# Up weights with turned signs: pair sums by additions and an adding DMA, h's operands moved by 128 bytes, and a cut second product

## The chip, the cores and the metric

The kernel runs on one core of a Trainium2 chip. The metric is the device time of one execution in microseconds (us), the median of several runs. A core has a matrix engine (TensorE, "PE" in the profile, with its weight loads as "PEld"), a vector engine (VectorE, "DVE"), a scalar engine (ScalarE, "ACT"), a general engine (GpSimd, "POOL") and a queue engine (SyncE, "SP") that issues plain DMAs. DMAs that add to what they find at their destination are issued by POOL here. Matrix products read two operands from on-chip memory (the loaded one is called "weights", the streamed one "moving") and write into one of eight accumulation banks.

## The reference

One layer of a bidirectional encoder on x of shape (1, 512, 1024), all in float32:

```python
x = x + 0.5 * swiglu(rms_norm(x, g1), w_gate1, w_up1, w_down1)   # 1024 -> 2752 -> 1024
h = rms_norm(x, g_mix);  u = h @ w_in
x = x + concat([fourier(u), attention(u)]) @ w_out
x = x + 0.5 * swiglu(rms_norm(x, g2), w_gate2, w_up2, w_down2)   # 1024 -> 2752 -> 1024
y = rms_norm(x, g_final)
# swiglu(h, g, u, d) = (silu(h @ g) * (h @ u)) @ d
```

The change touches the two SwiGLU blocks only.

## The kernel before, in words

Every product of two float32 matrices is done with split operands. A value is cast to the engine's short float form (the high part), and what the cast lost is the low part. `product` issues three matmuls: high weights times high, high weights times low, low weights times high. So each weight tile costs a DMA, a cast for the high part (mostly on ACT, L147, L343, L352) and a subtraction for the low part (mostly on DVE, `lows`, L118).

`ffn` does one SwiGLU block. The 2,752 hidden columns are 21 chunks of 128 and a tail of 64. Chunks are worked in four groups. The first group uses plain products on all 512 positions. In the other three groups, `seven` computes the gate and the up product of a chunk together as a "pair", by a scheme of seven half-size products instead of eight. The two weight matrices of the pair make a 2 by 2 block matrix (a11 and a12 are the upper and lower half of the gate chunk's 1,024 rows, a21 and a22 those of the up chunk), and the activations make another (b11, b12, b21, b22: halves of rows and of positions). The scheme needs four sums of weight blocks (s1 to s4) and four of activation blocks (t1 to t4, made once by `operands` and kept in `rt`). Each of the seven steps multiplies one weight block with one activation block: 4 row chunks times 3 split products are 12 matmuls of 128x128 weights with 256 moving columns, so a pair is 84 matmuls, all recorded at line L382 (`multiply`). Steps run in the order 0 (a11, bank r), 1 (a12, bank p2), the previous pair's step 9 (a22, its bank r), 3 (s1, bank q), 4 (s2, bank r), 5 (s4, bank q), 6 (s3, bank r). Between steps ACT copies partial results out of the banks (p1, p5, u2 by `kept`, L390; u at L418 and L426), applies silu (L414), and DVE adds and multiplies (L403, L413, L419, L427). The last pair's step 9 has no following pair; it is run by `rest` after the first down product of the group and is called the tail step below.

`prepare` makes the weights of a pair one pair ahead. It issues the DMAs of the gate and the up chunk (512 KB each) and returns a list of pieces: `both` casts two blocks into a high and a low slot, `single` does one block, and `combine` makes one of the four sums on DVE (L358). `PIECES` says how many pieces are handed out after each step. Weights live in a ring of 12 slots of 128x1024: eight of them (`own`) belong to the pairs in these stages, four (`shared`) also serve the down weights. A slot is taken by `take` and given back after the last step that reads it. `take(most)` prefers the own slots, except that for the last but one preparation of a stage it prefers the shared ones for everything but a11/a12.

After the pair stage of a group, `down` multiplies the finished activations (tile `at`) with eight tiles of down weights (products of 512 columns, L155 to L157), and `residual` (L468) adds each result to x. The first pair of the next group is prepared during these down products.

PE and SP execute in program order (`in_order`). On ACT, DVE and POOL a scheduler chooses the order when the kernel is built. All waits follow from who reads and writes a tile or a slot.

Lines to know: `ffn` 250 to 542, `operands` 296, `take` 319, `prepare` 330, `multiply` 376, `step` 393, the loop with the hand-out of pieces 432 to 445, `down` 447, the group loop 473 to 542. `room(pool, n)` places the next tile of a pool at address n modulo 256 bytes; the ring lies at 128, `at` at 128, `rt` at 192.

Of the kernel before, what the change touches and what calls it, by code (L numbers as in the profile page):

```python
# [6 lines left out]
F32 = mybir.dt.float32  # L7
# [6 lines left out]
P = 128  # L14
# [16 lines left out]
USES = "a11", "a12", "s1", "s2", "s4", "s3", "a22"  # L31
PIECES = (0, 2, 2, 1, 1, 1, 1)
KH = KD // 2
HI_DVE = ("f0", "f1")
SWAP_DMA = ("q1", "q2", "q3")
# [44 lines left out]
def encoder(ctx, tc, A, out):  # L80
# [169 lines left out]
    def ffn(norm, after, wgu, wd, wdt, groups, opening, closing):  # L250
# [6 lines left out]
        with tc.tile_pool(name=f"act{n_}", bufs=1) as ap, tc.tile_pool(name=f"sums{n_}", bufs=2) as sp:  # L257
            room(ap, 192)
            at = ap.tile([P, PLACES, 2, S], F32R, name=f"at{n_}")
            room(ap, 64)  # L260
            rt = ap.tile([P, 7, 2, KH, HALF], F32R, name=f"rt{n_}")
# [34 lines left out]
            def operands(rp, i0, i1):  # L296
                for i in range(i0, i1):
                    b = sp.tile([P, 4, HALF], F32, tag="raw_g", name=f"b{n_}_{i}")
                    for o, k in ((0, i), (2, i + KH)):
                        nc.vector.scalar_tensor_tensor(  # L300
                            out=b[:, o : o + 2].rearrange("p a b -> p (a b)"), in0=x[k],
                            scalar=gains[:, norm.n, k : k + 1], in1=rp, op0=ALU.mult, op1=ALU.mult,
                        )
                    b12, b11, b22, b21 = (b[:, o] for o in range(4))
                    t = sp.tile([P, 4, HALF], F32, tag=("s12", "s34")[i % 2], bufs=1, name=f"t{n_}_{i}")
                    for o, (p, q) in enumerate(((b12, b11), (b22, t[:, 0]), (b22, b12), (b21, t[:, 1]))):
                        nc.vector.tensor_tensor(out=t[:, o], in0=p, in1=q, op=ALU.subtract)
                    for src, c in ((b[:, 1:], slice(0, 3)), (t, slice(3, 7))):
                        h, l = rt[:, c, 0, i], rt[:, c, 1, i]
                        nc.scalar.copy(h, src)  # L310
# [18 lines left out]

            def prepare(j, most=False):  # L330

                g = sp.tile([P, KD * P], F32, tag="raw_g", name=f"raw_g{n_}_{j}")
                u = wp.tile([P, KD * P], F32, tag="raw", name=f"raw_u{n_}_{j}")
                for t, c in ((g, 2 * j), (u, 2 * j + 1)):
                    nc.sync.dma_start(out=t.rearrange("p (a b) -> p a b", b=P), in_=wgu[c])
                a11, a12, a21, a22 = g[:, :S], g[:, S:], u[:, :S], u[:, S:]
                s12 = sp.tile([P, 2 * S], F32, tag="s12", bufs=1, name=f"s12_{n_}_{j}")
                s34 = sp.tile([P, 2 * S], F32, tag="s34", bufs=1, name=f"s34_{n_}_{j}")
                w = {}

                def both(names, src):
                    hi, lo = (take(most and names[0] != "a11") for _ in range(2))
                    nc.scalar.copy(hi, src)  # L343
                    lows(lo, src, hi)
                    for i, n in enumerate(names):
                        w[n] = tuple(t[:, i * S : (i + 1) * S] for t in (hi, lo))
                    w[max(names, key=USES.index), "slots"] = hi, lo

                def single(n, src):
                    t = take(False)  # L350
                    hi, lo = t[:, :S], t[:, S:]
                    nc.scalar.copy(hi, src)  # L352
                    lows(lo, src, hi)
                    w[n] = hi, lo
                    w[n, "slots"] = (t,)

                def combine(out, a, b, op):
                    nc.vector.tensor_tensor(out=out, in0=a, in1=b, op=op)  # L358
# [12 lines left out]
            def seven(js, done):  # L371
# [3 lines left out]

                def multiply(ps, wn, on, w, first):

                    (whi, wlo), (mhi, mlo) = w[wn], (part[on][:, i] for i in range(2))
                    for i in range(KH):
                        ks = slice(i * P, (i + 1) * P)  # L380
                        for o, (a, b) in enumerate(((whi, mhi), (whi, mlo), (wlo, mhi))):
                            nc.tensor.matmul(  # L382
                                ps, a[:, ks], b[:, i], start=first and i == 0 and o == 0,
                                stop=i == KH - 1 and o == 2, skip_group_check=not first,
                            )
                    give(*w.get((wn, "slots"), ()))
# [6 lines left out]
                def step(j, w, n):  # L393
                    b = banks.setdefault(j, {})
                    if n == 0:
                        b["r"] = bank(f"r{n_}_{j}")[:, :HALF]
                        multiply(b["r"], "a11", "b11", w, True)
                        b["p1"] = kept(b["r"], "p1", j)
# [16 lines left out]
                    elif n == 6:  # L415
                        multiply(b["r"], "s3", "t3", w, False)
                        b["u"] = tp.tile([P, S], F32, tag="u", name=f"u{n_}_{j}")
                        nc.scalar.copy(b["u"][:, :HALF], b["r"])  # L418
                        nc.vector.tensor_tensor(  # L419
                            out=b["u"][:, :HALF], in0=b["u"][:, :HALF], in1=b["p5"], op=ALU.add  # L420
                        )
                    elif n == 9:
                        multiply(b["r"], "a22", "t4", w, False)
                        u, i = b["u"], place(j)
                        h, l = at[:, i, 0], at[:, i, 1]
                        nc.scalar.copy(u[:, HALF:], b["r"])  # L426
                        nc.vector.tensor_tensor(out=u, in0=b["g"], in1=u, op=ALU.mult)  # L427
# [4 lines left out]
                for s in range(7 * len(js)):  # L432
# [40 lines left out]
            for gi, group in enumerate(groups):  # L473
# [36 lines left out]
                for d in range(KD):  # L510
# [920 lines left out]
```

## Time and profile before

| what | value |
|---|---|
| runs shown | 856.64, 856.88, 858.42 us; median 856.88 |
| profiled execution, span from first to last instruction | 855.1 us, 1.8 below the median of the runs |
| granted TensorE clock, mean | 0.996 |
| PE busy | 846.4 us (99%) in 5,434 matmuls |
| DVE busy | 641.5 us (75%) |
| ACT busy | 467.9 us (55%) |
| POOL busy | 33.3 us (4%) |
| DMA | 89.25 MB, 28.6% of the engines on SP's queue, 3.2% on POOL's |
| matmuls of the pairs (L382) | 2,940 of 128x256, 381.5 us of records |
| matmuls of the down products (L155, L156, L157) | 900 of 128x512, 350.7 us of records |

The profile is that of one execution. Records of neighbouring matmuls overlap, because a matmul's record runs until its result is out while the next one has started; so the distance between two starts, not the length of a record, is the price of one matmul in a stream. A row of the timeline gives the start, the length and the operation, and `x12` means that twelve of them follow each other. Where an engine was idle before a row, the time and what ended it stand in brackets.

### The profile page before, as it was taken

How to read it: one execution, taken by the hardware profiler on the slowest of the kernel's cores; microseconds unless marked ns; L12 is line 12 of the kernel's file. 1: busy time of each engine (PE TensorE's matmuls, PEld its weight loads, DVE VectorE, ACT ScalarE, POOL GpSimd, SP SyncE). 2: the span in 40 equal slices, each digit the busy share in tenths (PEclk: the TensorE clock that was granted, in tenths of full speed). 3: DMA queues.
4: the chain of work that ended last, by engine and by line, in shares of the span. 5: the costliest groups of instructions: out<-in, count | busy, mean ns of one | idle time of the engine just before them, and what ended most of it. 6: DMA issues, size and time to landing. Idle time of an engine off the chain costs nothing.

```text
span 855.1 us, 13706 instructions
## 1 busy us (share of the span) xinstructions
PE 846.4 (99%) x5434; PEld 765.5 (90%) x5434; DVE 641.5 (75%) x1007; ACT 467.9 (55%) x781; POOL 33.3 (4%) x35
## 2 busy tenths in 40 slices
PE   9999999999999999999999999999999999999996
PEld 7878998899989998889988888899989998899986
DVE  7998985488756937699999478999846985488453
ACT  7763764266524635677776347656632764266352
POOL 0110000000000000222000000100000000000001
PEclk9999999999999999999999999999999999999998
DMA  6664322323243113414020224553232331323213
GB/s 250 164 157 157 118 88 74 118 99 127 74 145 109 48 56 111 148 50 136 26 74 26 99 70 116 120 196 108 77 117 100 118 106 56 117 100 113 67 43 99
DMA packets 31424, 89.25 MB, mean 104 GB/s; under 512 B 3712, under 2 KB 9344, under 8 KB 31232
## 3 DMA queue, kind: packets, MB, share of 16 engines
q1 hardware_dynamic: 28320, 82.87, 28.6%
q0 software_dynamic: 2496, 4.99, 3.2%
q8 instruction: 42, 0.69, 0.3%
q10 hardware_dynamic: 544, 0.52, 0.2%
q14 instruction: 22, 0.18, 0.1%
HBM read 83.91 MB, written 2.10 MB: 101 GB/s over the span
## 4 chain that ended last, share of the span: by engine, by line
PE 97%; DVE 1%; DMA 0%; issue 0%; ACT 0%; POOL 0%; POOLq 0%; DVEq 0%; ACTq 0%
PE r L382 23%; PE q L382 12%; PE dn L157 8%; PE dn L155 8%; PE dn L156 8%; PE p L382 6%; PE mix L155 3%; PE mix L157 3%; PE mix L156 3%; PE gu L632 3%; PE gu L155 2%; PE gu L157 2%; PE gu L156 2%; PE mix L1122 2%; PE mix L1079 2%; PE mix L928 1%
## 5 line engine op out<-in xcount | busy, mean ns | idle before, releaser
L382 PE MATMUL r<-rt,ring 128*128 128x256 f32 x1680 | 216.8, 280 | 0.0
L382 PEld LDWEIGHTS r<-rt,ring 128*128 128x128 f32 x1680 | 205.6, 188 | 2.6
L157 PE MATMUL dn<-at,ring 128*128 128x512 f32 x300 | 117.0, 390 | 0.5 <-DVE ring L118 0.5
L155 PE MATMUL dn<-at,ring 128*128 128x512 f32 x300 | 117.0, 390 | 0.0
L156 PE MATMUL dn<-at,ring 128*128 128x512 f32 x300 | 116.7, 389 | 0.0
L382 PE MATMUL q<-rt,ring 128*128 128x256 f32 x840 | 109.8, 279 | 0.0
L382 PEld LDWEIGHTS q<-rt,ring 128*128 128x128 f32 x840 | 103.5, 188 | 0.0
L468 DVE SCALAR_TENSOR_TENSOR gx<-dn,gx 128x512 f32<-128x512 f32 x61 | 42.0, 688 | 75.2 <-PE dn L157 75.2
L118 DVE TENSOR_TENSOR ring<-s,ring 128x1024 fp32r<-128x1024 f32 x70 | 85.3, 1220 | 16.5 <-PE r L382 10.5
L147 ACT CAST ring<-raw_dn 128x768 fp32r<-128x768 f32 (+3 forms) x58 | 45.5, 787 | 87.0 <-PE dn L156 70.6
L343 ACT CAST ring<-s 128x1024 fp32r<-128x1024 f32 x70 | 73.5, 1050 | 34.8 <-PE r L382 17.9
L157 PEld LDWEIGHTS dn<-at,ring 128*128 128x128 f32 x300 | 56.3, 188 | 13.0 <-DVE ring L118 1.1
L156 PEld LDWEIGHTS dn<-at,ring 128*128 128x128 f32 x300 | 56.3, 188 | 11.3
L155 PEld LDWEIGHTS dn<-at,ring 128*128 128x128 f32 x300 | 56.3, 188 | 11.3
L118 DVE TENSOR_TENSOR ring<-raw_dn,ring 128x768 fp32r<-128x768 f32 (+3 forms) x58 | 51.6, 892 | 6.1 <-ACT ring L147 4.1
L382 PE MATMUL p<-rt,ring 128*128 128x256 f32 x420 | 54.9, 279 | 0.0
L118 DVE TENSOR_TENSOR ring<-raw_g,ring 128x1024 fp32r<-128x1024 f32 x35 | 42.8, 1223 | 14.7 <-PE p L382 8.4
L382 PEld LDWEIGHTS p<-rt,ring 128*128 128x128 f32 x420 | 51.7, 188 | 0.0
L343 ACT CAST ring<-raw_g 128x1024 fp32r<-128x1024 f32 x35 | 36.8, 1051 | 21.5 <-DMA raw_g<-in_wgu 8.8
L352 ACT CAST ring<-raw_u 128x512 fp32r<-128x512 f32 x35 | 21.8, 622 | 33.5 <-PE dn L157 15.1
L427 DVE TENSOR_TENSOR u<-g,u 128x512 f32<-128x512 f32 x35 | 24.0, 686 | 16.0 <-ACT u L426 16.0
L224 POOL TENSOR_TENSOR r<-ms,mhalf 128x4 f32<-128x4 f32 (+1 forms) x5 | 5.9, 1179 | 679.9 <-DVE ms L217 679.9
(309 smaller groups left out, 1584.4 us busy)
## 6 DMA issues: line engine op xcount, KB each, us to landing
raw_g<-in_wgu SPq DMA_DIRECT2D x35, 512.0 KB, 3.7
raw_u<-in_wgu SPq DMA_DIRECT2D x35, 512.0 KB, 4.3
raw_dn<-in_wd SPq DMA_DIRECT2D x40, 384.0 KB, 3.1
raw_gu<-in_wgu SPq DMA_DIRECT2D x12, 512.0 KB, 3.6
raw_o<-in_wo SPq DMA_DIRECT2D x8, 512.0 KB, 3.5
raw_dn<-in_wd SPq DMA_DIRECT2D x8, 448.0 KB, 3.3
raw_wq<-in_wins SPq DMA_DIRECT2D x4, 512.0 KB, 4.6
raw_f<-in_winf SPq DMA_DIRECT2D x4, 512.0 KB, 3.5
```

The source lines that it names most:

```text
L118: nc.vector.tensor_tensor(out=lo, in0=src, in1=asf(hi), op=ALU.subtract)
L147: nc.scalar.copy(hi[:, :n, :], raw[:, :n, :])
L155: nc.tensor.matmul(ps, whi, mhi, start=first, stop=False)
L156: nc.tensor.matmul(ps, whi, mlo, start=False, stop=False)
L157: nc.tensor.matmul(ps, wlo, mhi, start=False, stop=last)
L343: nc.scalar.copy(hi, src)
L352: nc.scalar.copy(hi, src)
L382: nc.tensor.matmul(ps, a[:, ks], b[:, i], start=first and i == 0 and o == 0, stop=i == KH - 1 and o == 2, skip_group_check=not first,)
L427: nc.vector.tensor_tensor(out=u, in0=b["g"], in1=u, op=ALU.mult)
L468: nc.vector.scalar_tensor_tensor(out=x[d][:, t], in0=ps[:, t], scalar=0.5, in1=x[d][:, t], op0=ALU.mult, op1=ALU.add)
L632: nc.tensor.matmul(pss[c], w[:, k % 2, c], m[k], start=k == 0 and m is hh and w is hi, stop=k == KD - 1 and w is lo,)
L1079: nc.tensor.transpose(pts[n][:, c * P : (c + 1) * P], prob[t, b, c][:, kc * P : (kc + 1) * P], ident)
```

## The change

The up chunk takes part with the opposite sign. Before, the weight sums were s1 = a21 + a22, s2 = s1 − a11, s3 = a11 − a21, s4 = a12 − s2; after, they are s1 = a21 + a22, s2 = s1 + a11, s3 = a11 + a21, s4 = a12 + s2. The sign is put right where the results are read (ACT copies with scale −1, DVE subtracts p5 instead of adding it), and the activation sums t1 to t4 in `operands` change their signs.

- In `prepare`, a tile `t` receives by two DMAs of SP the upper half of the gate chunk (256 KB) and the upper half of the up chunk (256 KB). A third DMA of SP loads the whole gate chunk (512 KB), POOL issues an adding DMA of the whole up chunk (512 KB) onto `t`, and a fourth DMA of SP loads a22 alone (256 KB). So `t` holds s3 and s1 without any vector instruction. Once these have been cast, two additions on DVE turn `t` in place into s4 and s2. The tile has the tag "s" with two buffers; before there were two tiles with one buffer each.
- `take` loses its argument: own slots first, then shared ones, at all times. `PIECES` becomes (0, 1, 1, 1, 2, 1, 0), with six pieces a pair instead of eight.
- The pair for the second group is prepared from down product 2 on instead of 1.
- `room(ap, 192)` ahead of `rt` instead of `room(ap, 64)`: `rt` starts at 64 modulo 256 instead of 192.
- The second matmul of the first step of the first pair of every stage is cut into one of 64 and one of 192 columns (`HEAD`, `cols`).

```diff
-PIECES = (0, 2, 2, 1, 1, 1, 1)
+PIECES = (0, 1, 1, 1, 2, 1, 0)
+HEAD = 64
...
-            room(ap, 64)
+            room(ap, 192)
             rt = ap.tile([P, 7, 2, KH, HALF], F32R, name=f"rt{n_}")
...
-                    t = sp.tile([P, 4, HALF], F32, tag=("s12", "s34")[i % 2], bufs=1, name=f"t{n_}_{i}")
-                    for o, (p, q) in enumerate(((b12, b11), (b22, t[:, 0]), (b22, b12), (b21, t[:, 1]))):
-                        nc.vector.tensor_tensor(out=t[:, o], in0=p, in1=q, op=ALU.subtract)
+                    t = sp.tile([P, 4, HALF], F32, tag="s", name=f"t{n_}_{i}")
+                    for o, (p, q) in enumerate(((b11, b12), (t[:, 0], b22), (b22, b12), (t[:, 1], b21))):
+                        if o % 2:
+                            nc.vector.scalar_tensor_tensor(
+                                out=t[:, o], in0=p, scalar=-1.0, in1=q, op0=ALU.mult, op1=ALU.subtract
+                            )
+                        else:
+                            nc.vector.tensor_tensor(out=t[:, o], in0=p, in1=q, op=ALU.subtract)
...
-            def take(most):
-                pool = (shared or own) if most else (own or shared)
+            def take():
+                pool = own or shared
...
-            def prepare(j, most=False):
+            def prepare(j):
                 g = sp.tile([P, KD * P], F32, tag="raw_g", name=f"raw_g{n_}_{j}")
+                t = sp.tile([P, KD * P], F32, tag="s", name=f"s{n_}_{j}")
                 u = wp.tile([P, KD * P], F32, tag="raw", name=f"raw_u{n_}_{j}")
-                for t, c in ((g, 2 * j), (u, 2 * j + 1)):
-                    nc.sync.dma_start(out=t.rearrange("p (a b) -> p a b", b=P), in_=wgu[c])
-                a11, a12, a21, a22 = g[:, :S], g[:, S:], u[:, :S], u[:, S:]
-                s12 = sp.tile([P, 2 * S], F32, tag="s12", bufs=1, name=f"s12_{n_}_{j}")
-                s34 = sp.tile([P, 2 * S], F32, tag="s34", bufs=1, name=f"s34_{n_}_{j}")
+                a11, a12, a22 = g[:, :S], g[:, S:], u[:, :S]
+                s3, s1 = s4, s2 = t[:, :S], t[:, S:]
+                gate, up = wgu[2 * j], wgu[2 * j + 1]
+                nc.sync.dma_start(out=s3.rearrange("p (a b) -> p a b", b=P), in_=gate[:, :KH])
+                nc.sync.dma_start(out=s1.rearrange("p (a b) -> p a b", b=P), in_=up[:, :KH])
+                nc.sync.dma_start(out=g.rearrange("p (a b) -> p a b", b=P), in_=gate)
+                nc.gpsimd.dma_start(out=t.rearrange("p (a b) -> p a b", b=P), in_=up, accum_op=ALU.add)
+                nc.sync.dma_start(out=a22.rearrange("p (a b) -> p a b", b=P), in_=up[:, KH:])
...
                     (both, ("a11", "a12"), g),
-                    (combine, s12[:, :S], a21, a22, ALU.add),
-                    (combine, s12[:, S:], s12[:, :S], a11, ALU.subtract),
-                    (both, ("s1", "s2"), s12),
+                    (both, ("s3", "s1"), t),
                     (single, "a22", a22),
-                    (combine, s34[:, :S], a11, a21, ALU.subtract),
-                    (combine, s34[:, S:], a12, s12[:, S:], ALU.subtract),
-                    (both, ("s3", "s4"), s34),
+                    (add, s2, s1, a11),
+                    (add, s4, a12, s2),
+                    (both, ("s4", "s2"), t),
...
+                def cols(i, o, entry):
+                    cuts = (0, HEAD, HALF) if entry and (i, o) == (0, 1) else (0, HALF)
+                    return [slice(*c) for c in zip(cuts, cuts[1:])]
...
-                        multiply(b["r"], "a11", "b11", w, True)
+                        multiply(b["r"], "a11", "b11", w, True, j == js[0])
...
-                        nc.scalar.copy(b["u"][:, :HALF], b["r"])
+                        nc.scalar.activation(b["u"][:, :HALF], b["r"], AF.Copy, scale=-1.0)
                         nc.vector.tensor_tensor(
-                            out=b["u"][:, :HALF], in0=b["u"][:, :HALF], in1=b["p5"], op=ALU.add
+                            out=b["u"][:, :HALF], in0=b["u"][:, :HALF], in1=b["p5"], op=ALU.subtract
                         )
...
-                        nc.scalar.copy(u[:, HALF:], b["r"])
+                        nc.scalar.activation(u[:, HALF:], b["r"], AF.Copy, scale=-1.0)
...
-                        done.append(prepare(js[i + 1], i + 1 == len(js) - 2))
+                        done.append(prepare(js[i + 1]))
...
-                    if d == 1 and not last:
+                    if d == (1 if gi else 2) and not last:
                         ready = prepare(groups[gi + 1][0] + 1)
```

More of the change, by code (lines that the diff above doesn't have):

```diff
@@ L349, in single @@
                 def single(n, src):
-                    t = take(False)
+                    t = take()
                     hi, lo = t[:, :S], t[:, S:]
@@ L374, in seven, with multiply @@
                 banks = {}
-                def multiply(ps, wn, on, w, first):
+                def cols(i, o, entry):
+                    cuts = (0, HEAD, HALF) if entry and (i, o) == (0, 1) else (0, HALF)
+                    return [slice(*c) for c in zip(cuts, cuts[1:])]
+                def multiply(ps, wn, on, w, first, entry=False):
                     (whi, wlo), (mhi, mlo) = w[wn], (part[on][:, i] for i in range(2))
@@ L381, in multiply @@
                         for o, (a, b) in enumerate(((whi, mhi), (whi, mlo), (wlo, mhi))):
[L382 to L385, printed above, removed]
+                            for c in cols(i, o, entry):
+                                nc.tensor.matmul(
+                                    ps[:, c], a[:, ks], b[:, i, c], start=first and i == 0 and o == 0,
+                                    stop=i == KH - 1 and o == 2, skip_group_check=not first or entry,
+                                )
                     give(*w.get((wn, "slots"), ()))
```

6 lines of the change are left out of this document (3 added, 3 removed).

## The prediction, made before the result was known

> **What bounds the kernel now.** I read the page's shares first, then the chain of waits, then TensorE (PE) stage by stage. From the page:
>
> ```profile
> span 855.1 us, 13706 instructions
> ...
> PE 846.4 (99%) x5434; PEld 765.5 (90%) x5434; DVE 641.5 (75%) x1007; ACT 467.9 (55%) x781; POOL 33.3 (4%) x35
> ...
> PE 97%; DVE 1%; DMA 0%; issue 0%; ACT 0%; POOL 0%; POOLq 0%; DVEq 0%; ACTq 0%
> ```
>
> PE is the path. Only two things can move the end: the pace at which PE starts products, and new gaps between them. The six pair stages (`seven`), by stretches, L382 alone:
>
> ```profile
> core 0: us, PE busy (x) PEld busy (x), PEclk, DMA share, GB/s
> 76.36:134.68 58.32, 58.32 (x491) 58.02 (x491) 1.00 0.29 100
> 168.91:227.19 58.28, 58.27 (x492) 58.02 (x491) 1.00 0.29 100
> 261.43:309.82 48.39, 48.38 (x408) 48.13 (x407) 1.00 0.28 90
> 561.99:618.89 56.90, 56.89 (x492) 56.51 (x491) 1.00 0.31 107
> 653.10:711.39 58.29, 58.28 (x492) 58.03 (x491) 1.00 0.29 100
> 745.62:803.91 58.29, 58.28 (x492) 58.03 (x491) 1.00 0.28 95
> sum 338.47, PE 338.43 PEld 336.74; mean PE 56.40 PEld 56.12
> ```
>
> Five stages of 492 products and one of 408 make 2,868, at 118.0 ns each. Four stages of equal length agree within 0.04 us; the fourth is 1.4 us shorter at the same granted clock. The timeline shows why (start, length, operation):
>
> ```profile
> 116.42 1.57 PE L382 MATMUL p<-rt,ring 128*128 128x256 f32 x12
> 126.32 1.58 PE L382 MATMUL p<-rt,ring 128*128 128x256 f32 x12
> ...
> 577.74 1.57 PE L382 MATMUL q<-rt,ring 128*128 128x256 f32 x12
> 577.86 1.05 ACT L343 CAST ring<-s 128x1024 fp32r<-128x1024 f32 x1 [0.97 <-PE r L382]
> 578.82 0.37 ACT L390 COPY u<-r 128x256 f32<-128x256 f32 x1
> 579.24 2.99 PE L382 MATMUL r<-rt,ring 128*128 128x256 f32 x24
> ...
> 601.31 1.52 PE L382 MATMUL p<-rt,ring 128*128 128x256 f32 x12
> 610.83 1.52 PE L382 MATMUL p<-rt,ring 128*128 128x256 f32 x12
> ```
>
> The same step of two neighbouring pairs lies 9.90 us apart (84 products, 117.9 ns each) early, and 9.52 us (113.3 ns) after 579. So one shape has two steady rhythms. The switch follows a stall: ScalarE (ACT) ran a cast ahead of the copy u2, and PE's step 6 waited for that copy. Such a stall stands in the first three pairs of every stage, 18 in all; 17 of them left the slow rhythm as it was.
>
> **The change, part by part.**
>
> *Rhythm.* `rt` moves by 128 bytes modulo 256, so h's operands lie 192 bytes off the weights instead of 64, and each stage's second product is cut in two. What that does to the rhythm no row shows. Lower end: all 2,868 products at 113.3 ns are 325.0 us, 13.5 less than 338.5 (stalls included). Upper end from these rows: all at 117.9 without stalls, 338.1 us, 0.4 less. A rhythm slower than any shown isn't excluded. I take the lower end: the same instructions kept 113.3 ns for 39 us, through a further stall, so weights and h can stream at it; what lacked was the phase, and both edits act on phase and on nothing else. The six extra products cost between 0 and 0.113 us each; I take 0.3 in all.
>
> *Sums.* The groups of a pair's vector and scalar work that the steps below use (busy us, mean ns of one | idle before):
>
> ```profile
> L118 DVE TENSOR_TENSOR ring<-s,ring 128x1024 fp32r<-128x1024 f32 x70 | 85.3, 1220 | 16.5 <-PE r L382 10.5 <-ACT ring L343 5.6
> L343 ACT CAST ring<-s 128x1024 fp32r<-128x1024 f32 x70 | 73.5, 1050 | 34.8 <-PE r L382 17.9 <-PE p L382 15.6 <-DVE s L358 0.8
> ...
> L358 DVE TENSOR_TENSOR s<-s,raw_g 128x512 f32<-128x512 f32 x35 | 24.0, 687 | 0.6
> ...
> L358 DVE TENSOR_TENSOR s<-raw_g,s 128x512 f32<-128x512 f32 x35 | 24.0, 684 | 0.2
> L414 ACT ACTIVATE g<-g 128x512 f32<-128x512 f32 x35 | 22.1, 632 | 15.2 <-DVE g L413 15.2
> ...
> L352 ACT CAST ring<-raw_u 128x512 fp32r<-128x512 f32 x35 | 21.8, 622 | 33.5 <-PE dn L157 15.1 <-DMA raw_u<-in_wgu 8.2 <-PE dn L156 7.8
> ...
> L418 ACT COPY u<-r 128x256 f32<-128x256 f32 x35 | 12.8, 365 | 3.3 <-PE r L382 3.3
> ```
>
> Two of four additions leave VectorE (DVE): 2 × 0.686 us per pair, 48 us in all, worth nothing at the end because PE is the path. Opposite signs (a copy with scale −1, a subtraction for an addition) keep engine and shape: nothing.
>
> *DMAs.* Per pair SP issues 256 + 256 + 512 + 256 KB instead of 2 × 512, and POOL one 512 KB adding transfer. Median us from issue to landing stand last:
>
> ```profile
> raw_g<-in_wgu SPq DMA_DIRECT2D x35, 512.0 KB, 3.7
> raw_u<-in_wgu SPq DMA_DIRECT2D x35, 512.0 KB, 4.3
> ...
> ring<-in_wgu POOLq DMA_DIRECT2D x3, 512.0 KB, 5.2
> ```
>
> The sums' two buffers come free when DVE has read s4,s2 of the pair before last, about 1.0 us into a pair; SP waits there with g and a22 behind, as it waited before for its buffers. Halves by +3.7, adding transfer +5.2: 9.9 us, or 0.4 into the next pair. Its cast can't begin before PE has left step 1 (its slot), 2.6 us into that pair. So 2.2 us of cover, and the adding transfer would have to take 7.4 us before it cost anything: 0. The cast of a22 now stands between p5 and u2 in ACT's order of every second and fourth pair. In the fourth pair it also stands before the cast of `at`. Issued with its group at 1.0 and 1.25 MB deep in the queue, a22 lands some 5.4 us later, an estimate: 4.3 for the second of two 512 KB transfers (raw_u), 0.6 for the last 0.25 MB (half of the 1.0 to 1.2 that raw_u lands after raw_g) and 0.5 for more issues: 6.4. Its cast 0.62, that of `at` 0.62 and the copy 0.37 end at 8.0, and step 6 wants u2 at 6 × 1.36 = 8.16: 0, at most 0.3 at each of five places. In the second pair only 0.62 + 0.37 follow: 0. Nothing else queues on POOL in the stages. Other hand-out places in `PIECES`, and the first pair's preparation one down product later, only shift work that is done pairs ahead: 0.
>
> *New waits at the ends of the stages.* `take(most)` goes, and with it the rule that kept late pieces off the slots of the down weights. In the changed order on ACT and DVE:
>
> ```profile
> 134.80 0.39 PE L155 MATMUL dn<-at,ring 128*128 128x512 f32 x1
> ...
> 138.88 0.84 ACT L147 CAST ring<-raw_dn 128x768 fp32r<-128x768 f32 x1 [2.15 <-PE dn L156]
> 138.90 1.58 PE L382 MATMUL r<-rt,ring 128*128 128x256 f32 x12
> 139.10 0.69 DVE L468 SCALAR_TENSOR_TENSOR gx<-dn,gx 128x512 f32<-128x512 f32 x1 [1.58 <-PE dn L157]
> 139.75 0.96 DVE L118 TENSOR_TENSOR ring<-raw_dn,ring 128x768 fp32r<-128x768 f32 x1
> 140.32 0.40 PE L155 MATMUL dn<-at,ring 128*128 128x512 f32 x1
> 140.52 0.37 ACT L426 COPY u<-r 128x256 f32<-128x256 f32 x1 [0.80 <-PE r L382]
> ```
>
> Before, PE went from pair stage to down product at 134.80 and from the tail step (138.90) to the next down product at 140.32 without a gap; an engine released by a step starts 0.20 us after the next step does (140.52). After:
>
> (a) Second stage of each FFN, first down weights. Their cast stands behind the copy of u that follows the stage's last product. Let D be the start that PE would have had, one step (1.36) after step 6 began. The cast of s4,s2 gets its slot by the eleventh product of step 5, at D−1.36−0.11+0.20, so ACT runs it (1.05) to D−0.2, then silu (0.63) to D+0.4, the copy of u (0.37) to D+0.8, the down cast (0.84) to D+1.6; DVE's low part (0.96) follows to D+2.6. The first product waits to D+1.7, the third to D+2.65 instead of D+0.45: 2.2 lost. With ACT idle before the copy it is 0.20 + 0.37 + 0.84 + 0.96 + 0.05 − 0.45 = 2.0. Twice: 4.2 (4.0 to 4.4).
>
> (b) Second down weights in five stages: their slots hold the last pair's a22, which the tail step (start S) reads until its eleventh product. In the first stage of FFN1 only the low part's slot is held, but DVE does residual 0.69, low part of the third weights 0.96, then this one 0.96: from S+0.2 to S+2.8, against S+1.36+0.45 = S+1.8 when PE's third product wants it: 1.0. In the three others of six parts the slot comes free at S+1.45 (1.36 − 0.11 + 0.20); cast 0.84, low part 0.96, ready at S+3.3: 1.5 each. Later down products stay ahead of PE, since one takes 4.1 us and its cast and low part 1.8. FFN2's last has seven parts, so cast and low part together take about 7/6 of 1.80, an estimate: 1.8. Together 7.3; I allow 5.5 to 8, since which DVE operation is in the way at that moment is my reading.
>
> (c) FFN2's first down stage, products of 1.8 us each:
>
> ```profile
> 545.24 2.36 DVE L118 TENSOR_TENSOR rt<-t,rt 128x1024 fp32r<-128x1024 f32 x2 [0.63 <-ACT rt L310]
> 556.50 0.39 PE L155 MATMUL dn<-at,ring 128*128 128x512 f32 x1
> ```
>
> The first pair's sums wait for the first of these low parts (546.4), so they land at 546.4 + 3.7 + 5.2 = 555.3. ACT has their cast (1.05) ahead of the sixth down weights' (0.41), DVE their low part (1.22) ahead of that one's (0.42): 558.1, against 556.95 for PE's third product. 1.2 lost; between 0.4 (only the cast late) and 1.8. FFN1's first down stage has the same order with eleven matmuls to a product instead of eight, more cover by 0.7 us each: 0.
>
> *Sum.* −13.5 + 0.3 + 4.2 + 7.3 + 1.2 = −0.5 us: a span of 854.6. The median of the runs (856.88) lies 1.8 us above the profiled span, so 856.4. With the terms' ends it is 853.5 to 860.
>
> **Rivals.**
>
> *The rhythm stays (slower).* PE enters each stage from 512-column products, as now, and falls into 117.9 ns. Then −0.4 + 0.3 + 12.7 = +12.6: 869.5. For it: every entry in the trace and 17 of 18 stalls ended there; against it: 579 to 619. It decides as soon as fewer than nine tenths of the products run at 113.3, for each tenth is 1.3 us. The Trainium skill ("SBUF — State Buffer", Who interferes with whom) says that TensorE's read ports for weights and moving operand are independent and that it waits on nobody; by that rule offset and cut could change nothing, which is this rival. This trace's two rhythms for one shape (117.9 and 113.3 ns) bear it out only in part.
>
> *The rhythm is won and lost again (slower).* One gap in a stage, such as a22's cast ahead of u2 in its second or fourth pair, resets the phase. Half of the products at each rhythm: +6, 863.
>
> *Faster.* ACT or DVE gets to the new pieces sooner than the order by rows makes it: (b) at 1.0 each and (a) at 1.5 are 8.0, with (c) at 0.4 it is −13.2 + 8.4 = −4.8: 852.1. For it: (b)'s places rest on my reading of two queues; against it: (a)'s chain has no slack in its 2.0.
>
> **How the numbers follow.** No change in the median is 856.88; 0.2% (1.7 us) is about what a measurement here can tell from none. The forecast has 0.40, the rhythm lost midway 0.17, unchanged 0.20, faster 0.18, and 0.05 lies above 870 (a third, slower rhythm). The forecast's own 853.5 to 860 splits into 0.12 faster, 0.20 the same and 0.08 slower. So faster 0.30, same 0.20, slower 0.50. Range 852 to 870: some 0.1 below and 0.07 above left out.
>
> **What would show it.** Right: steps of one name 9.52 us apart from a stage's first pair on; gaps of some 2 us ahead of the first down product's third matmul in two stages and 1 to 1.8 us at the second's in five, with the low-part subtraction as releaser; no ACT wait ahead of step 6. Wrong: steps 9.90 apart, PE waiting for the adding transfer's cast, or down products that follow without gaps.

## The result, and the profile after

The changed kernel takes 876.75 us (median of four runs, 875.92 to 879.05) against 856.82 before. The ratio is 1.0227 with a 95% interval of 1.0208 to 1.0246: slower by 2.3%, outside the predicted 852 to 870. The profiled execution has a span of 875.0 us, 19.9 more than before. The page of the changed kernel:

```profile
span 875.0 us, 13923 instructions
...
PE 843.4 (96%) x5440; PEld 756.8 (86%) x5440; DVE 606.8 (69%) x937; ACT 468.4 (54%) x781; POOL 62.5 (7%) x70
...
PE 76%; DMA 9%; DVE 6%; ACT 4%; issue 2%; SPq 2%; POOL 0%; POOLq 0%; DVEq 0%; ACTq 0%
...
L396 PE MATMUL r<-rt,ring 128*128 128x256 f32 x1686 | 212.8, 279 | 12.5 <-ACT u L404 12.4
```

PE is busy for 3 us less than before, and yet it is no longer the whole path: 24% of the chain now runs through DMA, DVE, ACT and queues. The r products have idle time ahead of them, 12.4 us of it ended by ACT's copy u2 (L404). The six pair stages again, L396 alone:

```profile
core 0: us, PE busy (x) PEld busy (x), PEclk, DMA share, GB/s
77.58:136.48 58.90, 56.61 (x492) 56.05 (x492) 1.00 0.67 180
171.64:229.94 58.30, 56.37 (x492) 55.97 (x492) 1.00 0.56 147
267.78:316.30 48.52, 47.24 (x408) 46.84 (x408) 1.00 0.44 118
570.63:629.72 59.09, 56.35 (x492) 55.96 (x492) 1.00 0.74 190
665.55:726.05 60.50, 57.95 (x492) 57.55 (x492) 0.97 0.55 142
763.90:822.08 58.18, 56.36 (x493) 55.97 (x492) 1.00 0.49 128
sum 343.49, PE 330.89 PEld 328.34; mean PE 55.15 PEld 54.72
```

Before, length and busy time were equal in every row. Now the busy time is 7.5 us lower in all, and the stretches are 5.0 us longer, because 12.6 us of gaps stand in them. Between the gaps the products run in the fast rhythm: from the second product of each stage on they start 113.3 ns apart. Only in FFN1's third stage a small stall at 305.01 leads back, and its last hundred products are 117.8 ns apart.

From the starts of the first and the last product of each stage the 19.9 us can be booked. Inside the stages: 492 or 408 products at 113.3 ns would be 13.0 us less than before; 5.0 us more were measured; so gaps, with the slow restart after each and what they did to rhythm and clock, cost 18.0 us. From the end of the stages to the start of what follows: 0.94, 3.61, 1.61, 3.61 and 1.77 us longer than before, in the order first and second stage of FFN1, first, second and last of FFN2: 11.5. Ahead of FFN1's first stage 1.2, and between FFN1's last stage and FFN2's first 2.2 longer. −13.0 + 18.0 + 11.5 + 3.4 = 19.9.

One gap of the 18 us, in the fourth pair of the first stage (timeline: start, length, operation; in brackets the idle time before it and what ended it):

```profile
106.40 0.33 SPq L344 DMA_DIRECT2D s<-in_wgu  x1
106.77 0.43 SPq L345 DMA_DIRECT2D s<-in_wgu  x1
107.25 0.43 SPq L346 DMA_DIRECT2D raw_g<-in_wgu  x1
107.74 0.42 SPq L348 DMA_DIRECT2D raw_u<-in_wgu  x1
...
110.98 0.37 ACT L404 COPY p<-q 128x256 f32<-128x256 f32 x1 [0.57 <-PE q L396]
112.14 1.52 PE L396 MATMUL q<-rt,ring 128*128 128x256 f32 x12
114.35 0.62 ACT L362 CAST ring<-raw_u 128x512 fp32r<-128x512 f32 x1 [3.00 <-DMA raw_u<-in_wgu]
114.88 0.61 ACT L442 CAST at<-u 128x512 fp32r<-128x512 f32 x1
115.40 0.37 ACT L404 COPY u<-r 128x256 f32<-128x256 f32 x1
115.81 0.62 PE L396 MATMUL r<-rt,ring 128*128 128x256 f32 x3 [2.15 <-ACT u L404]
```

The pair starts at 105.34. SP gets the buffer of the sums at 106.40 and issues four transfers 0.4 to 0.5 us apart, so a22's (raw_u) goes out at 107.74. It lands 6.6 us later. ACT stands idle for 3.0 us, with its next instruction being a22's cast; then come the cast of `at` and only then u2, which PE needs for its next step since 113.50. Over the whole kernel ACT waits in this way in 11 places, the second and fourth pairs of the stages:

```profile
ACT ring L362 <- DMA raw_u<-in_wgu: 18.9, 11, 3.0
```

The end of a stage, FFN1's second:

```profile
230.27 0.37 ACT L432 ACTIVATE u<-r 128x256 f32<-128x256 f32 x1
230.53 0.82 ACT L148 CAST ring<-raw_dn 128x768 fp32r<-128x768 f32 x1
...
231.39 0.96 DVE L119 TENSOR_TENSOR ring<-raw_dn,ring 128x768 fp32r<-128x768 f32 x1
231.41 0.50 PE L156 MATMUL dn<-at,ring 128*128 128x512 f32 x1 [1.19 <-ACT ring L148]
232.40 0.50 PE L158 MATMUL dn<-at,ring 128*128 128x512 f32 x1 [0.26 <-DVE ring L119]
...
236.16 1.58 PE L396 MATMUL r<-rt,ring 128*128 128x256 f32 x12
...
237.66 0.83 ACT L148 CAST ring<-raw_dn 128x768 fp32r<-128x768 f32 x1 [0.69 <-PE r L396]
...
238.52 0.96 DVE L119 TENSOR_TENSOR ring<-raw_dn,ring 128x768 fp32r<-128x768 f32 x1 [0.56 <-ACT ring L148]
238.54 0.50 PE L156 MATMUL dn<-at,ring 128*128 128x512 f32 x1 [0.80 <-ACT ring L148]
...
239.53 0.50 PE L158 MATMUL dn<-at,ring 128*128 128x512 f32 x1 [0.26 <-DVE ring L119]
```

Both chains of the prediction are there. The first down weights' cast follows the copy of u, and their low part follows the cast. The second ones' cast starts 1.50 us after the tail step's start (236.16), when a22's slot comes free, and their low part is read at 239.53, 3.37 us after that start (the prediction had 1.45 and 3.3).

### The profile page after: what moved, and what is told of

Read it like the earlier page. It is cut to its first block, busy times and chain, and to the rows that moved or that the text cites. A ratio compares the mean times of both kernels' runs of the same rounds, so it can differ in the third digit from the quotient of the medians.

```text
span 875.0 us, 13923 instructions
## 1 busy us (share of the span) xinstructions
PE 843.4 (96%) x5440; PEld 756.8 (86%) x5440; DVE 606.8 (69%) x937; ACT 468.4 (54%) x781; POOL 62.5 (7%) x70
## 3 DMA queue, kind: packets, MB, share of 16 engines
q1 hardware_dynamic: 38400, 92.05, 33.2%
## 4 chain that ended last, share of the span: by engine, by line
PE 76%; DMA 9%; DVE 6%; ACT 4%; issue 2%; SPq 2%; POOL 0%; POOLq 0%; DVEq 0%; ACTq 0%
PE r L396 14%; PE dn L158 8%; PE dn L157 7%; PE dn L156 7%; DMA raw_u<-in_wgu 7%; PE q L396 6%; PE p L396 4%; DVE ring L119 4%; PE mix L156 3%; PE mix L158 3%; PE mix L157 3%; PE gu L156 3%; PE gu L157 2%; PE gu L158 2%; ACT ring L353 2%
## 5 line engine op out<-in xcount | busy, mean ns | idle before, releaser
L396 PE MATMUL r<-rt,ring 128*128 128x256 f32 x1686 | 212.8, 279 | 12.5 <-ACT u L404 12.4
L396 PEld LDWEIGHTS r<-rt,ring 128*128 128x128 f32 x1686 | 202.4, 189 | 16.0 <-ACT u L404 15.1
L158 PE MATMUL dn<-at,ring 128*128 128x512 f32 x300 | 117.8, 393 | 3.4 <-DVE ring L119 3.4
L396 PE MATMUL q<-rt,ring 128*128 128x256 f32 x840 | 106.7, 276 | 0.0
L396 PEld LDWEIGHTS q<-rt,ring 128*128 128x128 f32 x840 | 100.5, 188 | 0.0
L347 POOL DMA_DIRECT2D s<-in_wgu x35 | 30.1, 861 | 466.9 <-DVE ring L119 199.8
L396 PE MATMUL p<-rt,ring 128*128 128x256 f32 x420 | 53.6, 277 | 0.0
L396 PEld LDWEIGHTS p<-rt,ring 128*128 128x128 f32 x420 | 50.6, 189 | 0.0
L362 ACT CAST ring<-raw_u 128x512 fp32r<-128x512 f32 x35 | 21.7, 621 | 38.0 <-DMA raw_u<-in_wgu 18.9
L119 DVE TENSOR_TENSOR ring<-raw_u,ring 128x512 fp32r<-128x512 f32 x35 | 24.1, 688 | 16.1 <-ACT ring L362 13.8
```

Of the source, the lines that this page charges most:

```text
L119: nc.vector.tensor_tensor(out=lo, in0=src, in1=asf(hi), op=ALU.subtract)
L158: nc.tensor.matmul(ps, wlo, mhi, start=False, stop=last)
L347: nc.gpsimd.dma_start(out=t.rearrange("p (a b) -> p a b", b=P), in_=up, accum_op=ALU.add)
L396: nc.tensor.matmul(ps[:, c], a[:, ks], b[:, i, c], start=first and i == 0 and o == 0, stop=i == KH - 1 and o == 2, skip_group_check=not fi ...
```

## The experiments

Every run below is a kernel of its own. The change, b_off_head, boh_p4 and a_most were executed four times, the others once; the kernel before, executed beside them in four series, has medians of 856.82 to 858.48 us. "Stages" and "rest" are the differences to the kernel before, in us, of the six pair stages (first to last product) and of all the rest, from the profiled executions.

| run | time | stages | rest |
|---|---|---|---|
| the change | 876.75 | +5.0 | +14.9 |
| b_off | 849.13 | −8.2 | +0.5 |
| b_head | 857.62 | +0.8 | 0.0 |
| b_off_head | 853.45 | −3.9 | +0.2 |
| bo_p4 | 854.27 | −2.0 | −0.6 |
| bh_p4 | 856.51 | −1.3 | +1.0 |
| boh_p4 | 844.06 | −13.0 | +0.2 |
| b_nomost | 870.17 | +5.6 | +7.8 |
| a_most | 907.51 | +46.1 | +5.0 |
| a_dvesums | 857.57 | −10.2 | +10.9 |
| a_a22first | 873.97 | +2.5 | +14.6 |
| a_last1 | 864.75 | −4.4 | +12.0 |
| a_noadd | 878.79 | +8.7 | +13.3 |

### The rhythm: offset and cut, apart and together

`room(pool, n)` puts n bytes ahead of the pool's next tile. `at` lies at 128 modulo 256 and fills whole multiples of 256 bytes, so 64 bytes put `rt` at 192, and 192 bytes put it at 64. On the kernel before:

```diff
-            room(ap, 64)
+            room(ap, 192)          # b_off, b_off_head
...
-    multiply(b["r"], "a11", "b11", w, True)
+    multiply(b["r"], "a11", "b11", w, True, j == js[0])   # b_head, b_off_head: cut of 64 and 192 columns
...                                     # HEAD, cols and the loop over the cuts as in the change
```

> The kernel before with rt at 64 modulo 256 and no cut. Theory A (the offset decides alone): 113.3 ns a product as with both edits, 8 to 12 us less. Theory B (the offset only permits, the cut sets the phase at the start of a stage): the slow rhythm of 117.8 ns up to the first stall, and perhaps another one after it; within 3 us of the kernel before. A third, slower rhythm above 118 ns would show as a longer time.

> The kernel before with the second product cut and rt left at 192 modulo 256. Theory A (the offset decides alone): slow rhythm of 117.8 ns, time as before within 1 us. Theory B (the cut sets the phase): 113.3 ns at least until the first stall; after it either rhythm, as after 579 us in the kernel before: 3 to 12 us less.

> The kernel before with only the two rhythm edits: rt at 64 modulo 256, and the second product of each stage cut into 64 and 192 columns. Theory (the two edits alone set the phase, whatever prepares the weights): same steps of neighbouring pairs 9.52 us apart from the first pair on, the stalls of the first three pairs stay or grow a little (ScalarE still casts s3,s4 ahead of u2), and VectorE with 9.72 us of work per pair may add up to 0.2 us a pair: span down by 8 to 12 us, 843 to 847. Rival (the rhythm needs the other sums too): 9.90 us apart, within 1 us of the kernel before.

The offset alone gave 849.13, more than both together (853.45; ratio 0.9944, interval 0.9929 to 0.9959). The start of the first stage in b_off:

```profile
81.49 1.58 PE L382 MATMUL r<-rt,ring 128*128 128x256 f32 x12
82.91 1.58 PE L382 MATMUL q<-rt,ring 128*128 128x256 f32 x12
84.40 3.01 PE L382 MATMUL r<-rt,ring 128*128 128x256 f32 x24
87.25 1.52 PE L382 MATMUL p<-rt,ring 128*128 128x256 f32 x12
88.61 1.52 PE L382 MATMUL r<-rt,ring 128*128 128x256 f32 x12
```

The stage begins in the slow rhythm (steps 1.42 us apart, records of 1.58) and leaves the first stall (84.40) in the fast one (1.36, 1.52). All six stages of b_off do so, and none falls back at a later stall. With offset and cut every stage starts fast, but in four of six the third stall threw it back to 117.8 ns for good, and in a fifth the first stall did so for one pair. With the cut at the old offset (b_head) every stage starts slow; in three of them the first stall led to the fast rhythm and a later one back. So neither of the two expectations for the offset holds as it was put. Only with both edits does a stage enter fast, and what a stall does follows from neither edit alone.

To have no stalls, the pieces of the kernel before were handed out at other places, which in ACT's order moves the cast of s3,s4 behind u2:

```diff
-PIECES = (0, 2, 2, 1, 1, 1, 1)
+PIECES = (0, 2, 2, 0, 1, 1, 2)    # boh_p4: with offset and cut; bo_p4: offset alone; bh_p4: cut alone
```

> The kernel before with the two rhythm edits and the pieces handed out as (0, 2, 2, 0, 1, 1, 2), so that in ScalarE's order the cast of s3,s4 comes after u2 instead of before it. Theory (with the cut a stage starts at 113.3 ns and, without a stall that can flip the phase, stays there): 9.52 us a pair throughout, 842 to 845. Rival (VectorE's 9.7 us a pair stalls PE by itself, and the stall flips the rhythm back): 117.8 ns after some pairs, 848 to 854.

> As the kernel before with offset, cut and the pieces' places (0, 2, 2, 0, 1, 1, 2), which ran at 844, but without the cut. Theory (entering a stage from 512-column products gives the slow rhythm, and without a stall nothing ends it): 117.8 ns throughout, 856 to 858. Rival (at this offset the slow rhythm decays by itself or at any small gap): 113.3 ns from some pair on, 845 to 852.

> The same with the cut but with rt left at 192 modulo 256. Theory (the cut reaches the fast rhythm only at the new offset; at the old one every stage began at 117.8 ns with the cut too): 117.8 ns throughout, 856 to 858. Rival (the slow start there was an accident of the first stall): 113.3 ns in some stages, 845 to 854.

With both, the stages of boh_p4:

```profile
76.83:132.63 55.80, 55.79 (x493) 55.79 (x492) 1.00 0.30 105
...
sum 325.47, PE 325.41 PEld 325.26; mean PE 54.24 PEld 54.21
```

325.5 us are what 2,868 products take at 113.3 ns (325.0), and the prediction's lower end. The time is 844.06 (843.12 to 844.33), a ratio of 0.9829 with an interval of 0.9813 to 0.9845: faster than both kernels. Vector work of 9.7 us a pair (a pair's groups of the kernel before, summed) does not hold PE up in stages of five or six pairs, so the fast rhythm doesn't need the adding DMA. With only one of the two edits five of six stages keep 117.8 ns from end to end; the sixth has one remaining stall and goes fast after it. Their 854.27 and 856.51 are near the 857.27 of the kernel before beside them. Offset and cut are needed together where there is no stall.

### The slots

```diff
-                        done.append(prepare(js[i + 1], i + 1 == len(js) - 2))
+                        done.append(prepare(js[i + 1]))       # b_nomost: own slots first, on the kernel before
```

> The kernel before with own slots first at all times, nothing else. Theory (the slots held by the last pair's a22 make the waits at the second down products): 1.0 to 1.8 us in each of five stages, 7 us, and less than the 4.4 us of the changed kernel at the first down products, because ScalarE's order has their cast ahead of u2 here: 863 to 867. Rival (the waits need the adding scheme's late transfers): within 2 us of the kernel before.

The rest grew by 7.8 us, by 0.96, 1.61, 1.62, 1.61 and 1.83 at the ends of the five stages: part (b) of the prediction, with no adding DMA in the kernel. The 3.61 of the changed kernel at two of these places is this 1.61 and another 2.0, which is part (a). The time is 870.17, above the forecast 863 to 867, because stalls in the stages also rose by 5.6 us (six waits of PE for u2 together 3.6 us).

In the changed kernel, `take(most)` was put back:

```diff
-            def take():
-                pool = own or shared
+            def take(most):
+                pool = (shared or own) if most else (own or shared)   # a_most
...                                     # and the argument at the calls of take and prepare
```

> The changed kernel with the old take(most) put back, nothing else. Theory (the waits at the stages' ends come from the slots): the gaps ahead of the first and second down products, 11.4 us by the trace of the changed kernel (down stages 0.9, 3.6, 1.6, 3.6 and 1.7 us longer than before), go; ScalarE's order loses a22's cast ahead of u2 in the fourth pairs but keeps it in the second ones, so of the 18 us of stalls inside the stages some 10 go as well: 853 to 858. Rival (the adding transfers slow everything that is loaded, slots matter little): at most 4 us less, 871 or more.

The rest fell to +5.0 as the theory has it: at the ends of the stages nothing was left (differences of at most 0.13 us). But the time rose to 907.51 (ratio 1.0574, 1.0556 to 1.0591). What PE, and then ACT, waited for in this kernel:

```profile
PE r L396 <- ACT u L432: 32.6, 10, 5.9
PE r L396 <- ACT u L404: 5.0, 5, 1.2
```
```profile
ACT ring L353 <- DMA s<-in_wgu: 33.2, 10, 3.9
...
ACT ring L353 <- issue: 21.7, 4, 6.5
```

With other slots the scheduler put the cast of s3,s1 ahead of the copy of u, and that cast waited 33.2 us in ten places for the transfers into `t`, of which the adding DMA is the last. In four more places, 21.7 us together, the profile names nothing that ended the wait of this line. One of these ended at 126.55, 8.9 us after the issue of an adding DMA (117.70); PE's longest wait for u, 5.9 us, stands behind it. Neither theory had that. It is the same mechanism at another place: an instruction that waits for a late transfer holds up all that stands behind it on ACT. Not all of the 46.1 us is waiting: PE's granted clock was 0.94 to 0.97 in the six stages, and 0.50 for 2.3 us after that longest wait.

### Why the stages have gaps

All sums on DVE again, with gate and up loaded whole; signs, slots, offset and cut as changed, and the two sums handed out with the piece for a11,a12:

```diff
-PIECES = (0, 1, 1, 1, 2, 1, 0)
+PIECES = (0, 3, 1, 1, 2, 1, 0)          # a_dvesums
...
-                nc.sync.dma_start(out=s3.rearrange("p (a b) -> p a b", b=P), in_=gate[:, :KH])
-                nc.sync.dma_start(out=s1.rearrange("p (a b) -> p a b", b=P), in_=up[:, :KH])
                 nc.sync.dma_start(out=g.rearrange("p (a b) -> p a b", b=P), in_=gate)
-                nc.gpsimd.dma_start(out=t.rearrange("p (a b) -> p a b", b=P), in_=up, accum_op=ALU.add)
-                nc.sync.dma_start(out=a22.rearrange("p (a b) -> p a b", b=P), in_=up[:, KH:])
+                nc.sync.dma_start(out=u.rearrange("p (a b) -> p a b", b=P), in_=up)
...
+                    (add, s3, a11, a21),
+                    (add, s1, a21, a22),
                     (both, ("s3", "s1"), t),
```

> The changed kernel with all four sums on VectorE: gate and up chunk are loaded whole (2 x 512 KB), the two first sums are vector additions into the same tile t, no adding DMA; signs, slots, offset and cut as changed. Theory (the stalls of 18 us inside the stages come from the late landing of what the adding scheme loads, by way of ScalarE's order): they go, and the gaps of 11 us at the stages' ends stay: 856 to 862, steps of one name 9.52 us apart except where VectorE (9.7 us of work a pair) is late. Rival (the stalls come from the shared tile t and the single pieces' order): 872 or more.

857.57: the scheme of loading, with the order on ACT that goes with it, costs 19.2 us, all but 0.7 of the change's loss. The stages come to −10.2, near the −13.0 of a run without gaps, the 11 us at their ends stay, and the 3.4 us ahead of the first stages go. The order on ACT is not the changed kernel's: a22's cast stands ahead of p5 here, and the cast of `at` behind u2. So this run alone doesn't tell the landing from the order.

Which part of the scheme? First, the adding DMA left out, so that `t` keeps the two loaded halves and not the sums:

```diff
-                nc.gpsimd.dma_start(out=t.rearrange("p (a b) -> p a b", b=P), in_=up, accum_op=ALU.add)   # a_noadd
```

> The changed kernel without the adding DMA (the tile t then holds only the two loaded halves, so the sums and the output are not the reference's); ScalarE's order is the same as in the changed kernel, with a22's cast ahead of u2 in the second and fourth pairs. Theory (the adding packets share the DMA engines with the last packets of a22 and hold them up): a22 lands about 1 to 1.5 us earlier, at 6.3 to 7 us into the pair; the stalls in the stages fall from 18 us to under 5; 860 to 864. Rival (the four plain transfers alone land that late, by their number and the gaps between their issues): stalls within 4 us of the changed kernel, 872 to 877.

The theory fell: 878.79, a little above the rival's range too. PE waited 12.4 us in ten places for u2 in the changed kernel and 11.9 us in ten without the adding DMA:

```profile
PE r L395 <- ACT u L403: 11.9, 10, 2.4
```

The transfers of one pair (from issue to landing, the second stage's second pair), first the changed kernel, then a_noadd, then a_dvesums in the same stage:

```profile
s<-in_wgu SPq DMA_DIRECT2D x2, 256.0 KB, 3.6
raw_g<-in_wgu SPq DMA_DIRECT2D x1, 512.0 KB, 6.0
s<-in_wgu POOLq DMA_DIRECT2D x1, 512.0 KB, 5.4
raw_u<-in_wgu SPq DMA_DIRECT2D x1, 256.0 KB, 6.1
```
```profile
s<-in_wgu SPq DMA_DIRECT2D x2, 256.0 KB, 3.3
raw_g<-in_wgu SPq DMA_DIRECT2D x1, 512.0 KB, 5.7
raw_u<-in_wgu SPq DMA_DIRECT2D x1, 256.0 KB, 5.9
```
```profile
raw_g<-in_wgu SPq DMA_DIRECT2D x1, 512.0 KB, 3.8
raw_u<-in_wgu SPq DMA_DIRECT2D x1, 512.0 KB, 4.6
```

a22 lands 5.9 us after its issue even when nothing is added; two whole transfers land after 3.8 and 4.6. The issue matters more. In a_dvesums this chunk goes out 0.8 us before the second pair starts (174.27, the pair at 175.03), in the changed kernel 2.5 us into it (182.49, at 179.95), behind the wait for the buffer of `t` and three other issues. Its cast starts 3.9 us into the pair against 8.7; of these 4.8 us, 3.3 are the later issue and 1.5 the slower transfer. What the missing adding DMA did take away is the 2.2 us ahead of FFN2's first stage (part (c)): −0.1 there.

Second, the order on ACT, with all transfers kept:

```diff
-                    (single, "a22", a22),
                     (add, s2, s1, a11),
                     (add, s4, a12, s2),
                     (both, ("s4", "s2"), t),
+                    (single, "a22", a22),      # a_last1, with PIECES = (0, 1, 1, 0, 2, 1, 1)
```

> The changed kernel with a22's piece at the end of the list and the pieces handed out as (0, 1, 1, 0, 2, 1, 1): all DMAs as changed, but in ScalarE's order nothing but the cast of the activations stands ahead of u2. Theory (a late a22 costs only because u2 waits behind its cast): the 18 us of stalls in the stages go, the 11 us at the stages' ends and 3.4 us at the first stages' starts stay: 857 to 862. Rival (the adding DMA's sums themselves land too late, whatever ScalarE does first): PE then waits for the casts of s3,s1, 868 or more.

864.75, and the ten waits for u2 are down to one of 0.6 us; the stages come to −4.4. That is 9.4 of the 18 us. The other half is not simply gone: with a22's piece elsewhere PE waits for other copies, 2.7 us for u (L432) and 1.2 for p1 or p5, and in three stages the last one or two pairs fall to 117.8 ns. The forecast of 857 to 862 was too good by 3 us.

Third, a22's transfer moved ahead of the other three of its pair:

```diff
                 gate, up = wgu[2 * j], wgu[2 * j + 1]
+                nc.sync.dma_start(out=a22.rearrange("p (a b) -> p a b", b=P), in_=up[:, KH:])   # a_a22first, the old line gone
```

> The changed kernel with one line moved: the DMA of a22 is issued first of a pair's transfers instead of last. Theory (ScalarE waits with u2 behind a22's cast, and a22 lands 7.4 to 8.9 us into the pair): it lands some 3.5 us after the first issue, 4.7 us into the pair, before u2 is due; of 18 us of stalls at most 4 stay: 860 to 866. Rival (the transfers as a whole are too many, whichever goes first; what moves ahead delays s3,s1 and the adding DMA behind it): within 4 us of 876.8, with PE waiting for another cast.

873.97: the rival. PE's waits for u2 fell from 12.4 us in ten places to 4.9 in five, but the scheduler took the earlier transfer for a reason to put the cast still further forward, into first and third pairs, and ACT waited for it more than before:

```profile
ACT ring L362 <- DMA raw_u<-in_wgu: 41.2, 12, 7.3
```

In the changed kernel the same wait is 18.9 us in 11 places. In a_a22first PE also waited for p1 (2.2 us), and in three stages the fast rhythm was lost for a pair or more. So what costs is the pair of an order on ACT that was fixed when the kernel was built and a landing that is later than that order supposes; moving one of them moved the other.

## Why the prediction was wrong, point by point

**Rhythm: right, with luck in it.** It was taken at the lower end, 325.0 us; nearly all products outside the gaps ran at it, and boh_p4, which has no gaps, took 325.5. In an order without stalls both edits are needed, as bo_p4 and bh_p4 show; that what they set is a phase fits the runs, but none shows it. That the trace's stall at 579 reached the fast rhythm at the old offset was read rightly as a sign that it can be held. That it lasted through the changed kernel's gaps had no reason behind it: a_noadd, with gaps in the same pairs, lost it for some two pairs or more in five of six stages. The rival "rhythm stays" is excluded. What the prediction drew there from the Trainium skill's page "SBUF — State Buffer" (Who interferes with whom), that offset and cut could change nothing, fails in this case: they moved the same products from 117.8 to 113.3 ns. What in the memory or the engine makes the two rhythms no run shows.

**(a) and (b): right.** Forecast 4.2 and 7.3, 11.5 together; measured 0.94 + 3.61 + 1.61 + 3.61 + 1.77 = 11.5. b_nomost showed the slots as the cause of (b) by itself. The fence of the second stage shows (a)'s chain step by step.

**(c): mechanism right, size off.** Forecast 1.2 (0.4 to 1.8) and 0 for FFN1's first down stage; measured 2.2 and 1.2. In FFN2 the halves and the adding DMA took some 1 us longer to land than the rows of before gave: 9.9 us from the first issue (552.95) to the cast (562.82), against 8.9. a_noadd shows the adding DMA as the cause in FFN2; in FFN1 the 1.2 us stayed without it, and a_dvesums, which has neither adding nor separate halves, has −0.6 there.

**The cast of a22 ahead of u2: the step that failed.** The place was named, second and fourth pairs, and put at "0, at most 0.3 at each of five places". It measured 18.0 us. Two terms of it were too small. SP has three transfers to issue before a22's, 0.4 to 0.5 us each as a rule, so in the eleven places the issue is 2.4 to 3.5 us into the pair and not some 1.5. The cast starts 4.0 to 6.6 us after it, and not 4.9. That makes a cast at 7.5 to 9.0 instead of 6.4, with step 6 due at 8.16 and 1.6 us of ACT work between. And the second pairs, for which the prediction said 0 because only 0.62 + 0.37 follow, have gaps of 0.1 to 1.3 us; those of the fourth pairs are 0.6 to 2.2. Below it lies a wrong sentence: that SP waits for the sums' buffers "as it waited before for its buffers". The timeline of before shows the last up chunk of FFN1's second stage:

```profile
211.56 0.33 SPq L335 DMA_DIRECT2D raw_u<-in_wgu  x1
...
223.53 0.62 ACT L352 CAST ring<-raw_u 128x512 fp32r<-128x512 f32 x1
```

It was issued 12 us ahead of its cast, in the pair before. Not every chunk had such a lead: one issued at 173.50 was cast at 177.89, as soon as it had landed, after 1.9 us of idle time on ACT, and PE had no gap there. In the changed kernel, behind the sums' buffers, a22 is issued 2.4 to 3.5 us into the pair in which it is cast. A single estimate with less than 0.2 us of margin (8.0 against 8.16), of a kind that the trace could not show, carried eleven places, and got an upper end of 0.3 at five of them where a microsecond of delay in the transfer would have been paid in full.

**The rivals.** "Won and lost again" had the place right (a gap at a22's cast in the second or fourth pair) and the price wrong: in the changed kernel the fast rhythm outlived all eleven gaps, and the gaps themselves were the cost.

**Sums on DMA.** Two groups of sums (24.0 us each) are gone from DVE as forecast, a21 + a22 and a11 − a21; the prediction's fence shows the other two, which cost the same and stay. DVE's busy time on the page falls by 35 us (641.5 to 606.8) rather than 48, because the page counts overlapping records once; the records' lengths, summed, fall by 46.5. It was worth nothing at the end. That DVE is full at the fast rhythm, the worry of two expectations, was without ground: boh_p4 runs at it with the old vector work.

## What to carry to other kernels

Price a moved transfer by its place in the issuing queue, by what that queue waits for ahead of it, and by its landing under the new load; and where an in-order engine has an instruction that waits for it, pay the whole delay for everything behind that instruction. If a stream of equal products shows two steady distances between starts, try operand offsets and the way the stream is entered first: here an operand offset and one cut product, with an order that leaves no stall, gave 1.7% without touching the work, and the scheme meant to relieve the vector engine was not needed for it.

## What was not expected of the hardware

The offset of 128 bytes (modulo 256) between weights and moving operand changed what a stall does: at the new offset and without the cut each of the first stalls in six stages led from 117.8 to 113.3 ns, and none of the later ones led back; with the cut, five of the six stages lost the fast rhythm at some stall. At the old offset with the cut, the first stall led to it in three stages of six, and a later one back. What tells these stalls apart stays open.

After one gap, in FFN2's second stage (1.83 us idle until 704.03), PE's granted clock fell to half for some 3 us (windows of L396: length, PE busy, PEld busy, then the granted clock):

```profile
704.00:705.60 1.60, 1.57 (x12) 1.57 (x13) 0.92 1.00 197
705.66:707.00 1.34, 1.34 (x8) 1.34 (x8) 0.50 0.12 21
707.00:709.00 2.00, 2.00 (x12) 2.00 (x12) 0.56 0.52 150
```

From 705.66 to 708.65 the products start 213 ns apart instead of 113. That is some 1.6 of the 18 us. The longer gap of the first stage (the fence above, 2.15 us idle) had no such effect, so the length of the gap alone doesn't decide it.

From the first issue of a chunk's transfers to the last landing, the four of a_noadd take 7.2 us for 1.25 MB (181.20 to 188.39) and the two of a_dvesums 5.0 us for 1 MB (173.85 to 178.88). Bytes alone don't explain that: they differ by a quarter, the times by four tenths. Whether it is the number of transfers or their rows of half the length was not tried.
